# Two memory stacks, split operand tiles and ten plain columns of the feed-forward layer in a two-layer block of parallel heads

## The chip, the cores and the metric

The kernel runs on one core of one Trainium2 chip. TensorE multiplies matrices into PSUM; VectorE (DVE), ScalarE (ACT) and GpSimd (POOL) do the elementwise work; DMAs are issued from the queues of SP, POOL and ACT, each in its order. The metric is the device time of one launch in microseconds, as the median of several runs. All numbers are float32; matmul operands are split into a high part (type fp32r) and a low remainder, so one product costs three matmuls (high x high, high x low, low x high).

## The reference, cut to what matters

Two layers over 1024 tokens of width 1024. Each layer mixes tokens with four parallel heads and then applies a feed-forward part with a causal convolution of length 3 in its gate. Changed is only the feed-forward part of the second layer, and what lies around it.

```python
def conv_ffn(h, w_up, conv_w, conv_b, w_down):
    a, b = jnp.split(h @ w_up, 2, axis=-1)          # 1024 -> 2 x 2816
    a = causal_dwconv(a, conv_w) + conv_b.astype(a.dtype)
    return (jax.nn.gelu(a, approximate=True) * b) @ w_down

def hybrid_layer(x, ...):
    h = rms_norm(x, g_pre_mix)
    p = h @ w_in
    ...                                             # four mixers: pool, retention, gating, delta rule
    x = x + rms_norm(y @ w_out, g_post_mix)
    h = rms_norm(x, g_pre_ffn)
    x = x + rms_norm(conv_ffn(h, ffn_w_up, ffn_conv_w, ffn_conv_b, ffn_w_down), g_post_ffn)
    return x
```

## The kernel before

The tokens are worked on in two halves of 512 (`h` 0 and 1), the 2816 columns of the gate in 22 tiles of 128, called f. The code writes instructions in an order and with priorities (`high_priority` moves a block ahead); a scheduler of the compiler lays out each engine's order from that beforehand, with a simulated timeline, and also assigns buffers and semaphores. Each engine then runs its list in order. A tile that reuses memory waits for the last users of that memory.

The second layer's feed-forward part is done in two forms.

*Plain form* (`plain_up`, L1038): an f of half 0 takes two column tiles of w_up through `a_unit` (L205), each 8 k-steps x 3 matmuls of 512 columns, then `conv_gate` (convolution, gelu, product). Six f (`NPRE`) are done so for half 0. Two of them (`NFILL`) are filled into `win`, the mixers of half 1, the other four stand after it, before the output projection `out` of half 1. Each result c is stored to DRAM (`gD`, L1046). `plain_down` (L1048) loads it again with the rows of w_down, splits both and multiplies all six in one accumulation, for half 0 alone, and stores the sum (`accD`, L1079).

*Seven-product form* (`up_f`, L1133): both column tiles of an f are one 2 x 2 block product of 512 x 512 blocks, done with seven products and some sums instead of eight. `build` (L1099) loads the normalised rows `hn` from DRAM (`hnD`), forms four sums on POOL (L1109 to L1112), transposes seven blocks on TensorE (L1117), and writes their high and low parts (L1120, L1121) into the tiles A11, S1, S2, A12, S3, Q4, A22. Each such tile holds both token halves side by side, 512 columns; `build` is called once per half, with two token pairs per call. `up_f` loads the weights (`wraw`, L1140), casts seven weight blocks (L1145, L1146, added up by L1150), runs seven times `product` (12 matmuls each, L1129 to L1131), and gates. With `halves` (0, 1) a matmul has 512 columns, with (1,) it takes the 256 of half 1. The store of c goes from SP's queue (L1203).

The order at the end of the kernel is: `win` of half 1 with the fill; four more plain f; `out` of half 1, which ends in `norms` (L310) and the stores of hnD from SP's queue (L324); `plain_down`; `build` of half 1; f 0 and 1 for half 1; `build` of half 0; then f 2 to 5 for half 1, each in turn with one of f 6 to 21 for both halves; `down_full` (L1205), which loads w_down and gD per f (L1215, L1217), splits them, and multiplies in six groups, with the first two groups for half 1 alone and the sum of `accD` added.

Working memory is one stack of pools. `phase` (L135) closes all of them and opens the next set: the mixers' pools, then those of the seven products (`up_phase`), then those of `down_full` (`down_phase`).

```python
self.phase(("pw", 3), ("pr", NR), ("pa", 4), ("py", 2), ("pt", 5), ("ph", 4), ("pp", 1))   # mixers, plain form
self.phase(("pv", 2), ("pu", 1), ("pA", 1))                                                # seven products
self.phase(("pa", 8), ("py", 12), ("pw", 2), ("pr", 2), ("pg", 6))                         # down_full
```

Here pw holds weights, pr rows of 4 KB (`r4`), pa accumulators, ph transposed rows, pp the mixers' tensors, pv the weights of the seven products, pu the tags c (6 buffers: hn, sa, sb, a, c) and p, pA the A tiles, pg the split operands of `down_full`.

## Time and profile before

| | |
|---|---|
| median of 3 runs | 2526.12 us (2523.63 to 2530.67) |
| the profiled execution | 2522.4 us, span 2520.6 us |
| mean granted TensorE clock | 0.981 |
| TensorE busy | 2423.0 us, 96% of the span, 14020 matmuls |
| VectorE busy | 1777.1 us, 71% |
| ScalarE busy | 971.6 us, 39% |
| GpSimd busy | 251.7 us, 10% |
| DMA | 281.33 MB, mean 112 GB/s |

Times within the profile are microseconds from the start of the span. An arrow names what is written and what is read (`psg<-whi,hT` writes PSUM tile psg from whi and hT). After a bar stand busy time and mean length, after a second bar the idle time of the engine ahead of the group and what ended it. PEld is the loading of weights into TensorE, which overlaps its matmuls; SPq, POOLq and ACTq are DMA issues. The seven products run from about 1900 to 2291, `down_full` from 2303 to the end.

### The profile page before, as it was taken

What the parts mean: (1) busy time and instruction counts of PE and PEld (TensorE: products, weight loads), DVE (VectorE), ACT (ScalarE), POOL (GpSimd) and SP (SyncE); (2) the same over time, 40 slices, a digit from 0 to 9 for tenths busy, and PEclk for the clock granted to TensorE, in tenths of its full rate; (3) what the DMA queues carried; (4) which work ended last, traced back from release to release, by engine and by line L of the source; (5) the groups of instructions that cost most, each with busy time, mean ns of one, the idle gap of its engine ahead of it and who ended that gap; (6) DMA issues with size and microseconds to landing.
All of it is one profiled execution on the core that took longest, in us unless ns stands there. A gap on an engine that the chain in (4) does not pass through costs nothing.

```text
span 2520.6 us, 36318 instructions
## 1 busy us (share of the span) xinstructions
PE 2423.0 (96%) x14020; PEld 2023.0 (80%) x14020; DVE 1777.1 (71%) x3659; ACT 971.6 (39%) x1510; POOL 251.7 (10%) x351
## 2 busy tenths in 40 slices
PE   8989998999999999899999999989888999998998
PEld 7968887877788987787778898877767888886887
DVE  8895699765655888955565589886567876664547
ACT  6333452423333453342332255233345444434212
POOL 2321103000000022200000001211003000000000
PEclk9999999999999999999999999999898999998999
DMA  5233343322233552222222355323363222215424
GB/s 185 72 90 111 126 135 92 103 80 76 80 100 109 161 166 84 76 94 77 84 84 85 124 167 188 92 82 110 117 226 118 101 92 83 77 59 201 141 67 151
DMA packets 100496, 281.33 MB, mean 112 GB/s; under 512 B 30482, under 2 KB 30802, under 8 KB 99812
## 3 DMA queue, kind: packets, MB, share of 16 engines
q1 hardware_dynamic: 96548, 266.37, 32.2%
q0 software_dynamic: 3776, 12.65, 1.5%
q8 instruction: 110, 1.80, 0.3%
q14 instruction: 62, 0.51, 0.1%
HBM read 239.11 MB, written 39.88 MB: 111 GB/s over the span
## 4 chain that ended last, share of the span: by engine, by line
PE 77%; DVE 14%; DMA 3%; issue 3%; ACT 2%; POOL 0%; SPq 0%; DVEq 0%; ACTq 0%; POOLq 0%
PE psg L213 9%; PE psg L214 9%; PE psg L212 9%; PE psg L1286 3%; PE psg L1288 3%; PE psg L1287 3%; DVE pr L839 3%; PE psg L233 3%; PE psg L1129 3%; PE psg L1131 3%; PE psg L1130 3%; PE psg L234 3%; PE psg L235 3%; DVE wlo L203 2%; DVE A L841 2%
## 5 line engine op out<-in xcount | busy, mean ns | idle before, releaser
L212 PE MATMUL psg<-hT,whi 128*128 128x512 f32 x1248 | 496.4, 398 | 0.6 <-DVE rs L286 0.5
L213 PE MATMUL psg<-hT,whi 128*128 128x512 f32 x1248 | 496.4, 398 | 0.0
L214 PE MATMUL psg<-hT,wlo 128*128 128x512 f32 x1248 | 494.9, 398 | 0.0
L202 ACT CAST whi<-raw 128x1024 fp32r<-128x1024 f32 (+1 forms) x272 | 283.4, 1049 | 530.7 <-PE psg L213 217.8
L203 DVE TENSOR_TENSOR wlo<-raw,whi 128x1024 fp32r<-128x1024 f32 (+1 forms) x249 | 307.4, 1240 | 142.2 <-ACT whi L202 138.1
L213 PEld LDWEIGHTS psg<-hT,whi 128*128 128x128 f32 x1248 | 234.9, 188 | 54.5 <-issue 0.9
L214 PEld LDWEIGHTS psg<-hT,wlo 128*128 128x128 f32 x1248 | 235.0, 188 | 54.0 <-issue 0.4
L212 PEld LDWEIGHTS psg<-hT,whi 128*128 128x128 f32 x1248 | 235.2, 188 | 53.4 <-issue 1.3
L1293 DVE TENSOR_TENSOR acc<-acc,psg 128x512 f32<-128x512 f32 x160 | 108.9, 685 | 74.7 <-PE psg L1288 74.2
L1145 ACT CAST w<-wraw 128x512 fp32r<-128x512 f32 x154 | 92.7, 619 | 176.5 <-PE psg L1131 109.9
L234 PE MATMUL psg<-wlo,hT 128*128 128x256 f32 (+1 forms) x512 | 148.7, 291 | 4.8 <-DVE wlo L203 4.3
L233 PE MATMUL psg<-whi,y 128*128 128x256 f32 x512 | 143.9, 286 | 6.5 <-DVE raw L1018 2.8
L233 PE MATMUL psg<-whi,hT 128*128 128x256 f32 (+1 forms) x512 | 146.4, 290 | 2.3 <-ACT tmp L434 1.1
L235 PE MATMUL psg<-whi,hT 128*128 128x256 f32 (+1 forms) x512 | 148.0, 290 | 0.0
L234 PE MATMUL psg<-wlo,y 128*128 128x256 f32 x512 | 144.0, 284 | 0.8 <-DVE rv L295 0.8
L235 PE MATMUL psg<-whi,y 128*128 128x256 f32 x512 | 142.7, 283 | 0.0
L1286 PE MATMUL psg<-whi,g 128*128 128x512 f32 x352 | 141.5, 404 | 0.0
L1146 DVE TENSOR_TENSOR w<-wraw,w 128x512 fp32r<-128x512 f32 x154 | 105.0, 696 | 51.1 <-ACT w L1145 50.6
L1287 PE MATMUL psg<-wlo,g 128*128 128x512 f32 x352 | 138.8, 394 | 0.0
L1288 PE MATMUL psg<-whi,g 128*128 128x512 f32 x352 | 138.6, 394 | 0.0
L839 DVE SCALAR_TENSOR_TENSOR pr<-A 64x1 f32<-64x1 f32 (+30 forms) x124 | 110.4, 890 | 8.6 <-POOL A L835 6.4
L234 PEld LDWEIGHTS psg<-wlo,hT 128*128 128x128 f32 x512 | 98.4, 192 | 8.5 <-DVE wlo L203 5.1
(488 smaller groups left out, 5151.4 us busy)
## 6 DMA issues: line engine op xcount, KB each, us to landing
raw<-in_wU SPq DMA_DIRECT2D x100, 512.0 KB, 3.5
raw<-in_wA SPq DMA_DIRECT2D x56, 512.0 KB, 3.5
raw<-in_wD SPq DMA_DIRECT2D x50, 512.0 KB, 3.6
wraw<-in_wU SPq DMA_DIRECT2D x22, 1024.0 KB, 4.9
raw<-in_wO SPq DMA_DIRECT2D x40, 512.0 KB, 3.7
raw<-in_wB SPq DMA_DIRECT2D x24, 512.0 KB, 3.6
xs<-xb SPq DMA_DIRECT2D x24, 512.0 KB, 3.5
graw<-gD SPq DMA_DIRECT2D x22, 512.0 KB, 4.5
```

The lines of the kernel that those rows point to most:

```text
L202: nc.scalar.copy(hi[:, :n], raw[:, :n])
L203: eng.tensor_tensor(lo[:, :n], raw[:, :n], hi[:, :n].bitcast(F32), ALU.subtract)
L212: nc.tensor.matmul(ps, a[0], b[0], start=first, stop=False)
L213: nc.tensor.matmul(ps, a[0], b[1], start=False, stop=False)
L214: nc.tensor.matmul(ps, a[1], b[0], start=False, stop=last)
L233: self.nc.tensor.matmul(ps[:, :width], h0, hi[:, s], start=k == 0, stop=False)
L234: self.nc.tensor.matmul(ps[:, :width], h0, lo[:, s], start=False, stop=False)
L235: self.nc.tensor.matmul(ps[:, :width], h1, hi[:, s], start=False, stop=k == len(hT) - 1)
L839: V.scalar_tensor_tensor(pr[:, 0:i, 0:i], A[:, 0:i, 0:i], -1.0, A[:, 0:i, i].unsqueeze(1).to_broadcast([64, i, i]), ALU.mult, ALU.mult)
L1286: nc.tensor.matmul(ps, hi[:, tb], us[i][0][:, s], start=i == 0, stop=False)
L1287: nc.tensor.matmul(ps, hi[:, tb], us[i][1][:, s], start=False, stop=False)
L1288: nc.tensor.matmul(ps, lo[:, tb], us[i][0][:, s], start=False, stop=i == len(g0) - 1)
```

## The change

- The working memory becomes two stacks, a left and a right one. `layout(side, ...)` closes and opens one of them, so the pools of the next stage come in while the other side still works. The tags c (4 buffers instead of 6) and the loaded weights (two tiles of half the size, 3 buffers in a tag of pu) shrink with it.
- Each A tile is split by token half; `product` issues one matmul of 256 columns per half in place of one of 512.
- Ten f instead of six take the plain form for half 0. A generator, `plain_part`, yields after each pair of f: two up products, their gate split at once into pr tiles (no way through gD), and the down products of the pair before, added up in four accumulators. One step runs in the fill, two before `out`, the remaining ones after `build` of half 1 has been written.
- The stores of hnD and of the c of `up_f`, and the loads of hn, go from POOL's queue.
- `down_full` loads only the second half of gD for the ten plain f and has seven groups. The descriptor area for POOL's DMAs is 4096 instead of 8192 bytes.

```diff
-NPRE, NFILL = 6, 2
+NPRE, NMIX = 10, 2
...
+    def layout(self, side, *pools):
+        stack = self.stacks.pop(side, None)
+        if stack is not None:
+            stack.close()
+        stack = self.stacks[side] = ExitStack()
         for name, bufs in pools:
-            p = self.tc.tile_pool(name=f"{name}{self.nphase}", bufs=bufs, reuse_waits="tile")
+            p = self.tc.tile_pool(name=f"{name}{self.nphase}", bufs=bufs, side=side, reuse_waits="tile")
...
     def mix_phase(self):
-        self.phase(("pw", 3), ("pr", NR), ("pa", 4), ("py", 2), ("pt", 5), ("ph", 4), ("pp", 1))
-
-    def up_phase(self):
-        self.phase(("pv", 2), ("pu", 1), ("pA", 1))
+        self.layout("right", ("pw", 3), ("pa", 4), ("pr", NR), ("ph", 4))
+        self.layout("left", ("py", 2), ("pt", 5), ("pp", 1))
 
     def down_phase(self):
-        self.phase(("pa", 8), ("py", 12), ("pw", 2), ("pr", 2), ("pg", 6))
+        self.layout("right")
+        self.layout("left", ("pa", 8), ("py", 2), ("pw", 2), ("pr", 2), ("pg", 6))
...
-                    nc.sync.dma_start(keep[b * P:b * P + P], hn[b])
+                    nc.gpsimd.dma_start(keep[b * P:b * P + P], hn[b])
...
+    def plain_part(self, l, hT):
         nc, V = self.nc, self.nc.vector
         self.accD = self.pd.tile([HALF, D], F32, name="accD")
+        acc = self.acc_tiles()
+
+        def down(fs, gs):
+            us = [self.unit(self.t["wD"][l, f]) for f in fs]
+            for b in range(NB):
+                tb = slice(b * P, b * P + P)
+                for n in range(2):
+                    s = slice(n * 512, n * 512 + 512)
+                    ps = self.ps()
+                    for i in range(len(fs)):
+                        hi, lo = gs[i]
+                        nc.tensor.matmul(ps, hi[:, tb], us[i][0][:, s], start=i == 0, stop=False)
+                        nc.tensor.matmul(ps, hi[:, tb], us[i][1][:, s], start=False, stop=False)
+                        nc.tensor.matmul(ps, lo[:, tb], us[i][0][:, s], start=False, stop=i == len(fs) - 1)
+                    with self.tc.high_priority(offset=1500):
+                        if fs[0] == 0:
+                            nc.scalar.copy(acc[b][:, s], ps)
+                        else:
+                            V.tensor_tensor(acc[b][:, s], acc[b][:, s], ps, ALU.add)
+                if fs[-1] == NPRE - 1:
+                    nc.sync.dma_start(self.accD[tb], acc[b])
+
+        prev = None
+        for f0 in range(0, NPRE, GRP):
+            self.up = UF
+            fs = list(range(f0, f0 + GRP))
+            gs = []
+            cc = self.r4("c")
+            for i, f in enumerate(fs):
+                pa = self.a_unit(self.t["wU"][l, 2 * f], hT)
+                pb = self.a_unit(self.t["wU"][l, 2 * f + 1], hT)
+                with self.tc.high_priority(offset=1500):
+                    c = cc[:, i * HALF:i * HALF + HALF]
+                    self.conv_gate(l, 0, f, c, pa, pb)
+                    g = self.r4("g", F32R)
+                    self.split(g[:, :HALF], g[:, HALF:], c)
+                gs.append((g[:, :HALF], g[:, HALF:]))
+            if prev is not None:
+                down(*prev)
+            prev = (fs, gs)
+            yield
+        down(*prev)
+        yield
...
-        return self.pu.tile([P, 1028], F32, tag="c", name=name, bufs=6)
+        return self.pu.tile([P, 1028], F32, tag="c", name=name, bufs=4)
...
-                nc.sync.dma_start(x[:, :D], self.hnD[l][r0:r0 + P])
+                nc.gpsimd.dma_start(x[:, :D], self.hnD[l][r0:r0 + P])
...
+    def product(self, ps, n, b, halves, first, last):
         for k in range(4):
             s = slice(k * P, k * P + P)
+            for i, (x, y) in enumerate(((0, 0), (0, 1), (1, 0))):
+                for j, h in enumerate(halves):
+                    self.nc.tensor.matmul(ps[:, 256 * j:256 * j + 256], b[:, x, s], self.A[h][n][y][:, k, :],
+                                          start=first and k == i == j == 0, stop=k == 3 and i == 2,
+                                          skip_group_check=not first or j > 0)
...
-        raw = self.pv.tile([P, 4, 512], F32, tag="raw", name="wraw")
+        rb, ra = (self.pu.tile([P, 2, 512], F32, tag="raw", name="wraw", bufs=3) for _ in range(2))
...
-        nc.sync.dma_start(self.gD[l][f, :, halves[0] * HALF:halves[0] * HALF + 2 * N], c)
+        nc.gpsimd.dma_start(self.gD[l][f, :, halves[0] * HALF:halves[0] * HALF + 2 * N], c)
...
-        groups = [[0, 1], [2, 3, 4, 5], [6, 7, 8, 9], [10, 11, 12], [13, 14, 15, 16], [17, 18, 19, 20, 21]]
+        groups = [[0, 1], [2, 3, 4], [5, 6, 7], [8, 9], [10, 11, 12, 13], [14, 15, 16], [17, 18, 19, 20, 21]]
...
-                nc.sync.dma_start(r, self.gD[l][f])
+                o = HALF if f < NPRE else 0
+                nc.sync.dma_start(r[:, o:], self.gD[l][f, :, o:])
...
             def fill(a=acc):
-                keep["hT"] = self.to_hT(a, True)
-                self.plain_up(l + 1, 0, range(NFILL), keep["hT"])
+                keep["g"] = self.plain_part(l + 1, self.to_hT(a, True))
+                next(keep["g"])
...
-        self.plain_up(l, 0, range(NFILL, NPRE), keep["hT"])
+        part = keep["g"]
+        for _ in range(NMIX):
+            next(part)
         self.out(l, 1, y, True)
-        self.plain_down(l)
-        self.up_phase()
-        self.rows(l)
+        self.A = {}
+        self.layout("left", ("pu", 1), ("pA1", 1))
+        self.rows(self.pA1, 1)
         self.build(l, 1)
-        self.up_f(l, 0, (1,), 0)
-        self.up_f(l, 1, (1,), 0)
+        for _ in part:
+            pass
+        self.layout("right", ("pA0", 1), ("pv", 9))
+        self.rows(self.pA0, 0)
+        for f in range(2):
+            self.up_f(l, f, (1,))
         self.build(l, 0)
...
-                   dynamic_dma_scratch_size=8192)
+                   dynamic_dma_scratch_size=4096)
```

More of the change, by code (lines that the diff above doesn't have):

```diff
@@ L1036, in conv_gate @@
         V.tensor_tensor(c, c, pb, ALU.mult)
-    def plain_up(self, l, h, fs, hT):
-        self.up = UF
-        for f in fs:
-            c = self.pa.tile([P, HALF], F32, tag="acc", name="c")
-            pa = self.a_unit(self.t["wU"][l, 2 * f], hT)
-            pb = self.a_unit(self.t["wU"][l, 2 * f + 1], hT)
-            with self.tc.high_priority(offset=1500):
-                self.conv_gate(l, h, f, c, pa, pb)
-            self.nc.sync.dma_start(self.gD[l][f, :, h * HALF:h * HALF + HALF], c)
@@ L1095, in build, with sums @@
-    def build(self, l, h):
+            self.A[h][n] = [pool.tile([P, 4, 256], F32R, tag=f"{n}{x}", name=f"{n}{x}{h}") for x in "hl"]
+    def sums(self, xs, bufs):
+        L, R = slice(0, 512), slice(512, 1024)
+        s1, s2, q4, s3 = bufs
+        G = self.nc.gpsimd
+        G.tensor_tensor(s1, xs[1][:, L], xs[1][:, R], ALU.subtract)
+        G.tensor_tensor(s2, s1, xs[0][:, L], ALU.subtract)
+        G.tensor_tensor(q4, s2, xs[0][:, R], ALU.add)
+        G.tensor_tensor(s3, xs[0][:, L], xs[1][:, L], ALU.subtract)
+        return (("A11", xs[0][:, L]), ("S1", s1), ("S2", s2), ("A12", xs[0][:, R]), ("S3", s3), ("Q4", q4),
+                ("A22", xs[1][:, R]))
@@ L1096, in build, with turned, put @@
+    def turned(self, p, x):
+        for k in range(4):
+            self.nc.tensor.transpose(p[:, k * P:k * P + P], x[:, k * P:k * P + P], self.ident)
+        return p.rearrange("p (k t) -> p k t", k=4)
+    def put(self, n, p4, h, i):
+        cs = slice(i * P, i * P + P)
+        hi, lo = self.A[h][n]
+        self.nc.scalar.copy(hi[:, :, cs], p4)
+        self.nc.vector.tensor_tensor(lo[:, :, cs], p4, hi[:, :, cs].bitcast(F32), ALU.subtract)
+    def build(self, l, h, pairs=(0, 1)):
         nc = self.nc
-        V, A = nc.vector, self.A
@@ L1098, in build @@
-        for i in range(2):
-            cs = slice(h * 256 + i * P, h * 256 + i * P + P)
+        for i in pairs:
             xs = []
@@ L1123, in product @@
-    def product(self, ps, a, b, cs, first, last):
-        nc = self.nc
-        ah, al = self.A[a]
+            for j, (n, x) in enumerate(self.sums(xs, (sa[:, 0:512], sa[:, 512:1024], sb[:, 0:512], sb[:, 512:1024]))):
+                self.put(n, self.turned((self.ps, self.pq)[j % 2](), x), h, i)
+    def product(self, ps, n, b, halves, first, last):
         for k in range(4):
             s = slice(k * P, k * P + P)
-            st, sk = first and k == 0, not first
-            nc.tensor.matmul(ps, b[:, 0, s], ah[:, k, cs], start=st, stop=False, skip_group_check=sk)
-            nc.tensor.matmul(ps, b[:, 0, s], al[:, k, cs], start=False, stop=False, skip_group_check=sk)
-            nc.tensor.matmul(ps, b[:, 1, s], ah[:, k, cs], start=False, stop=k == 3, skip_group_check=sk)
+            for i, (x, y) in enumerate(((0, 0), (0, 1), (1, 0))):
[3 more added lines that the diff above has]
+                                          skip_group_check=not first or j > 0)
@@ L1179, in up_f @@
             nc.gpsimd.tensor_copy(a[:, 0:2], cf[:, f, :])
-        self.product(X, "A11", w11, cs, True, False)
-        self.product(Z, "S1", wt1, cs, True, False)
+        self.product(X, "A11", w11, halves, True, False)
+        self.product(Z, "S1", wt1, halves, True, False)
         with self.tc.high_priority(offset=1500):
@@ L1184, in up_f @@
             nc.scalar.copy(p5, Z)
-        self.product(X, "S2", wt2, cs, False, False)
-        self.product(W, "A12", w21, cs, True, True)
+        self.product(X, "S2", wt2, halves, False, False)
+        self.product(W, "A12", w21, halves, True, True)
         with self.tc.high_priority(offset=1500):
@@ L1189, in up_f @@
             V.tensor_tensor(p1, p1, W, ALU.add)
-        self.product(X, "S3", wt3, cs, False, False)
-        self.product(Z, "Q4", w22, cs, False, True)
+        self.product(X, "S3", wt3, halves, False, False)
+        self.product(Z, "Q4", w22, halves, False, True)
         with self.tc.high_priority(offset=1500):
@@ L1194, in up_f @@
             V.tensor_tensor(at[:, :, 0], v(Z), v(u2), ALU.subtract)
-        self.product(X, "A22", wt4, cs, False, True)
+        self.product(X, "A22", wt4, halves, False, True)
         with self.tc.high_priority(offset=1500):
@@ L1385, in run @@
         self.down_full(l)
-        self.stack.close()
+        for st in self.stacks.values():
+            st.close()
 _SHAPES = dict(
```

98 lines of the change are left out of this document (24 added, 74 removed).

## The prediction, made before the changed kernel ran

> **What bounds the kernel now.** I read the page first, then the table of stretches, then the waits of the stretches where TensorE stands still, then single rows for prices.
>
> ```profile
> span 2520.6 us, 36318 instructions
> PE 2423.0 (96%) x14020; PEld 2023.0 (80%) x14020; DVE 1777.1 (71%) x3659; ACT 971.6 (39%) x1510; POOL 251.7 (10%) x351
> ...
> PE 77%; DVE 14%; DMA 3%; issue 3%; ACT 2%; POOL 0%; SPq 0%; DVEq 0%; ACTq 0%; POOLq 0%
> ```
>
> TensorE is the bound nearly everywhere (77% of the chain that ended last), so a change can gain in two ways: fewer matmuls, or fewer of the few places where TensorE waits. This change adds matmuls, so its case rests on the waits. In the table of stretches the columns are length, busy time of PE, PEld, DVE, ACT, POOL, granted clock, DMA share, GB/s:
>
> ```profile
> 1730.00:1770.00 40.00, 40.00 (x415) 31.20 (x414) 24.82 (x55) 15.83 (x35) 3.64 (x12) 1.00 0.37 122
> 1770.00:1800.00 30.00, 21.90 (x146) 18.08 (x144) 17.41 (x59) 5.95 (x11) 3.90 (x11) 0.72 0.16 53
> 1800.00:1840.00 40.00, 38.32 (x313) 37.31 (x312) 24.96 (x52) 21.67 (x35) 0.00 (x0) 1.00 0.65 215
> 1840.00:1880.00 40.00, 36.36 (x144) 27.42 (x144) 21.37 (x58) 14.05 (x23) 0.00 (x0) 0.96 0.61 213
> 1880.00:1900.00 20.00, 9.32 (x43) 7.34 (x41) 16.30 (x24) 10.52 (x20) 7.53 (x6) 0.70 0.60 223
> 1900.00:1925.00 25.00, 23.98 (x196) 23.58 (x196) 20.82 (x36) 13.80 (x27) 4.44 (x5) 0.97 0.19 64
> 1925.00:1945.00 20.00, 15.03 (x89) 13.24 (x90) 14.06 (x24) 10.18 (x18) 11.55 (x11) 0.83 0.42 159
> 1945.00:2000.00 55.00, 55.00 (x320) 47.90 (x320) 43.04 (x68) 26.61 (x48) 0.95 (x4) 1.00 0.27 97
> 2290.00:2304.00 14.00, 1.43 (x6) 0.85 (x5) 5.61 (x6) 3.73 (x5) 0.00 (x0) 0.64 0.45 150
> ```
>
> I count as lost in a stretch its length less busy time times clock, since an idle TensorE also comes back at a lower clock. 1770:1800, the end of the scan: 30 - 21.90 x 0.72 = 14.2 us. 1840:1880, the plain down products: 5.1. 1880:1900, the first build: 13.5. 1900:1945, first products and second build: 1.7 + 7.5 = 9.2. 2290:2304, the step from up to down: 13.1. Together 55 us; the steady stretches around them lose nothing. What ended the waits (us in total, times, longest):
>
> ```profile
> PE psh L971 <- DVE tmp L625: 4.8, 2, 3.4
> ...
> ACT wbig L207 <- DMA raw<-in_wD: 5.2, 2, 3.9
> ...
> PE psg L1117 <- DMA hn<-hnD: 9.6, 3, 7.3
> ...
> PEld psg L1117 <- ACT w L1145: 7.7, 1, 7.7
> ```
>
> ```profile
> PE psm L1235 <- ACT g L207: 12.6, 1, 12.6
> ...
> ACT g L207 <- DMA wraw<-in_wD: 9.8, 3, 7.5
> ```
>
> So: a latency chain between VectorE and TensorE at the end of the scan, then normalised rows that go out to DRAM and come back (hnD), then weight loads that come late.
>
> **The change part by part.** Prices of a matmul are distances between starts, not durations, since durations overlap. The first pair of rows is 36 matmuls of 512 columns apart, the second 51 of 256:
>
> ```profile
> 2091.87 0.39 PE L1129 MATMUL psg<-A11h,w 128*128 128x512 f32 x1
> ...
> 2100.27 0.39 PE L1129 MATMUL psh<-A12h,w 128*128 128x512 f32 x1
> ```
>
> ```profile
> 1915.10 0.28 PE L1129 MATMUL psg<-S2h,w 128*128 128x256 f32 x1
> ...
> 1921.10 0.28 PE L1129 MATMUL psh<-A12h,w 128*128 128x256 f32 x1
> ```
>
> 8.40 us / 36 = 233 ns, 6.00 / 51 = 118 ns.
>
> *More plain f.* The four f from 6 to 9 leave the seven-product form for half 0. A plain half f is 2 units x 8 k x 3 = 48 matmuls of 512: 11.2 us. Their seven-product form was 84 matmuls of 512 for both halves, 19.6 us; now 84 of 256 for half 1, 9.9 us, plus 11.2: +1.5 us each, +6.0. Down products per f and half stay 24 matmuls, 5.6 us.
>
> *Operand tiles by token half.* For the 12 f that still do both halves each of 84 matmuls of 512 becomes two of 256: 2 x 118 - 233 = +3 ns a pair, x 1008 = +3.0 us. TensorE's work therefore grows by 9.0 us, all on the path.
>
> The Trainium skill speaks harder against this part: "TensorE: Matmul & The Clock Gate", section "Back-to-back issue gap", gives for a stream with weight loads about 81 ns at 128 columns and 131 ns at 512. Halfway in proportion, an estimate of mine, that is 98 ns at 256, so 65 ns a pair and +65 us in all. The rows above, which have their weight loads between them, say 3 ns.
>
> *Downs before the scan ends.* The fill of before, up products of f 2 to 5, runs out at 1770; its last c is stored at 1771.5:
>
> ```profile
> L1046 SPq DMA_DIRECT2D gD<-c x6: 320/326/338, 1693.3 to 1771.5; - x6
> ```
>
> The generator now adds the downs of f 0 to 3, 4 x 5.6 = 22.4 us, ahead of the output projection and independent of the scan. That is more than the 14.2 us lost. But every TensorE step of the scan then queues behind a few of them, so the chain ends later, and downs are evacuated on VectorE (below), the engine of the chain. Bounds: -14.2 (all filled) and 0 (the chain stretches as much as is filled). I take -11, because the same scan in 1730:1770, with fill, lost nothing.
>
> *Plain f behind the output projection.* In 1840:1900 18.6 us are lost: the down products wait for wD, and the build of half 1 waits for hnD, for sums on POOL, and for casts. Now f 6 to 9 (44.8 us of up) and the downs of f 4 to 9 (33.6) stand there, 78.4 us that need nothing of the projection; the gate's output goes straight into the split, with no trip through gD. From the first down product, right behind the projection, to the first product of the new form
>
> ```profile
> 1840.32 0.77 PE L1075 MATMUL psg<-whi,g 128*128 128x512 f32 x2 [0.64 <-ACT whi L207]
> ...
> 1899.78 0.58 PE L1129 MATMUL psh<-A12h,w 128*128 128x256 f32 x1
> ```
>
> it took 60 us, so the cover is 18 longer than what it covers. If it were gone, the 18.6 would return. Bounds -18.6 and -9 (as if a second, uncovered wait for casts of 7.7 us stayed, since the nine w tiles lie in memory that the plain tiles leave late). I take -16.5.
>
> *Second build.* Four buffers of tag c instead of six hold hn, hn, sa, sb of one token pair, so the second pair waits for the first, and all wait for a and c of the two half-f before them. The new rows of half 0 also need the memory of the weights and accumulators of the last plain downs.
>
> ```profile
> 1921.81 0.32 SPq L1203 DMA_DIRECT2D gD<-c  x1
> 1922.23 1.28 SPq L1104 DMA_DIRECT2D hn<-hnD  x2
> ...
> 1930.72 0.32 SPq L1203 DMA_DIRECT2D gD<-c  x1
> ```
>
> ```profile
> xb<-xs SPq DMA_DIRECT2D x16, 512.0 KB, 3.7
> ...
> hn<-hnD SPq DMA_DIRECT2D x8, 512.0 KB, 5.8
> xb<-xs POOLq DMA_DIRECT2D x8, 512.0 KB, 4.7
> ...
> gD<-c SPq DMA_DIRECT2D x12, 256.0 KB, 2.0
> ```
>
> ```profile
> L1109 POOL TENSOR_TENSOR sa<-hn x4: 1269/1272/1542, 1888.9 to 1935.2; 128x512 f32<-128x512 f32 x4
> ...
> L1121 DVE TENSOR_TENSOR Q4l<-psg,Q4h x4: 673/686/691, 1897.6 to 1944.6; 128x512 fp32r<-128x512 f32 x4
> ```
>
> Before, the loads sat on SP's queue behind the store of c. Now both are on POOL's queue: a store waits for its c, and behind it queue the loads, the sums and the small writes into a. The last buffer comes free when the second c has left (1930.7 + 2.0, plus 1.0 for POOL's queue by the two xb rows: 1934), then two sums, transposes, the second load (5.8 + 1.0) and four sums of 1.27: about 1949, where before the last row was written at 1945.3. So this stretch may lose 4 us more. Against that, casts for these f may run ahead under the last downs (ahead=2000 instead of 0), so the clock is up when it starts. Bounds -9 and +12 (a second full load and sums in the open); I take +1.
>
> On that 1.0 us the Trainium skill, "DMA: Bandwidth & Descriptors", section "Specifications", has about 1 us against 0.6 to the first byte; by it three transfers in this chain would cost 1.2 us instead of 3.0.
>
> *Up to down.* This is SP's queue at the seam:
>
> ```profile
> 2282.23 1.21 SPq L1217 DMA_DIRECT2D graw<-gD  x2
> 2295.21 0.32 SPq L1203 DMA_DIRECT2D gD<-c  x1
> 2296.31 0.32 SPq L1217 DMA_DIRECT2D graw<-gD  x1
> 2296.68 8.28 SPq L1215 DMA_DIRECT2D wraw<-in_wD  x3
> ...
> L1129 PEld LDWEIGHTS psm<-S1h,w x88: 187/188/197, 1902.9 to 2272.9; 128*128 128x128 f32 x88
> ```
>
> wD for the down stage was issued behind the store of the last c, after all products. With the store on POOL, and the load's memory now lying over S1 and A11 of half 1 (by the sizes in the code), it can leave once S1's last matmuls (2272.9) are through, some 15 us before the seam. What is late next: g of the second f lies over Q4 and A22, so its casts start at the last product; six partial sums of the first f (6 x 3 x 0.233 = 4.2 us) stand before it, and the accumulators lie where c was. Loads of gD are halved for ten f. Bounds -13.1 and -3; I take -11.
>
> *Smaller things.* Plain downs in twos rather than one group of six give 40 evacuations instead of 8, 32 of them adds:
>
> ```profile
> L1293 DVE TENSOR_TENSOR acc<-acc,psg 128x512 f32<-128x512 f32 x160 | 108.9, 685 | 74.7 <-PE psg L1288 74.2
> ```
>
> 32 x 0.685 = 22 us of VectorE, spread over some 140 us at 60%: hidden, unless it meets the normalisation; +1.5 (0 to +5). hnD and gD stores leave SP's queue, which frees weight loads behind them: in the terms above. The smaller descriptor area I cost at nothing, as POOL's transfers are few; with stalls it would lengthen the second build.
>
> Sum: +9.0 - 11 - 16.5 + 1 - 11 + 1.5 = -27 us. The profiled execution took 2522.4, the median of the runs shown is 2526.1; so 2495 beside the former and about 2499 as a median.
>
> **The rivals.** (1) *All covered.* The waits vanish and the second build is hidden by f 2: -14.2 - 18.6 - 9.2 - 13.1 + 9 = -46, 2480. For it: cover exceeds the loss at each place. Against it: TensorE's order is fixed beforehand, and the old order, too, had work (f 2) that did not fill the second build. (2) *The wait moves.* The second build, now on one queue with stores and four buffers, costs the +12 of its bound, and the scan keeps its 14 us: 9 + 0 - 16.5 + 12 - 11 + 1.5 = -5, 2521. For it: the rows of POOL's queue above; against it: 9.9 us of f 2 can stand there. (3) *The downs do not cover.* They are placed, but the projection and the norms run behind them in TensorE's queue, so the chain is as late as before: only the seam is gained, -11 + 9 = -2, 2524, no measurable change. (4) *Slower:* the split matmuls. If the 256-column pairs do not run at 235 ns, because weight loads then set the pace, each ns costs 1.0 us. It decides from 235 + 27 = 262 ns a pair; at the 188 ns that one load lasts, unhidden once a pair, it gives 2499 + 190 = 2689. For it: twice the loads in twelve f; against it: the 51 matmuls above, loads included.
>
> The Trainium skill's numbers ("Back-to-back issue gap", as above) would put rival 4 at 2499 + 62 = 2561; the trace speaks for 235.
>
> **How the numbers follow.** My forecast (2486 to 2512) 0.60; (1) 0.12; (2) 0.11, of which 0.07 within 0.3%; (3) 0.06; (4) 0.05; an order on TensorE that I don't see, slower, 0.06. A measurement of this kernel tells 0.3%, 8 us, from no change. Faster 0.60 + 0.12 + 0.04 = 0.76; same 0.07 + 0.06 = 0.13; slower 0.11. The range that leaves out two in ten reaches from (1) to (2), 2480 to 2522.
>
> **What would show it.** Right: 256-column products about 118 ns apart and no 512-column ones; TensorE at clock 1.0 from the scan to the first product, with downs in it; casts of A rows of half 1 under plain matmuls; wD of the down stage issued before the last product, and a seam of some 2 us. Wrong: pairs well over 235 ns; a hole of more than 12 us before the first product that uses A rows of half 0; the same hole before the projection with downs on both sides of it.

## The result: 31 us slower, and the profile after

The changed kernel took 2556.6 us (median; 2554.5 to 2557.6) against 2525.9 us for the kernel before on the same chip: ratio 1.012, interval 1.010 to 1.0135. I had forecast 2499. The page of the changed kernel, to set beside the one shown before the prediction:

```profile
span 2555.8 us, 38925 instructions
PE 2435.4 (95%) x15220; PEld 2093.1 (82%) x15220; DVE 1809.1 (71%) x3719; ACT 983.0 (38%) x1538; POOL 272.0 (11%) x389
PEclk9999998999999999999999999999969899999999
PE 75%; DVE 14%; DMA 4%; issue 4%; ACT 2%; POOL 1%; SPq 0%; DVEq 0%; ACTq 0%; POOLq 0%
```

The same row of clocks in the kernel before:

```profile
PEclk9999999999999999999999999999898999998999
```

A new 6 stands in the row of clocks where there was none: behind a standstill of TensorE the granted clock was low. The table of stretches shows where (length, busy time of PE, PEld, DVE, ACT, POOL, granted clock, DMA share, GB/s):

```profile
1737.00:1806.00 69.00, 67.38 (x461) 53.74 (x461) 45.41 (x113) 27.53 (x51) 6.46 (x20) 1.00 0.21 69
1806.00:1858.00 52.00, 47.71 (x383) 46.75 (x382) 31.30 (x63) 26.08 (x41) 0.54 (x1) 0.97 0.58 194
1858.00:1887.00 29.00, 0.00 (x0) 0.00 (x0) 16.33 (x49) 5.81 (x9) 2.66 (x5) 0.57 0.72 248
1887.00:1907.00 20.00, 13.39 (x59) 11.50 (x60) 8.85 (x13) 7.94 (x14) 11.46 (x12) 0.60 0.17 56
1907.00:1985.00 78.00, 77.70 (x337) 62.94 (x335) 40.61 (x53) 20.07 (x29) 0.00 (x0) 1.00 0.24 81
1985.00:2011.00 26.00, 21.73 (x166) 20.09 (x166) 21.79 (x39) 12.60 (x25) 1.65 (x3) 1.00 0.39 131
2011.00:2036.00 25.00, 12.45 (x61) 9.76 (x62) 19.05 (x27) 10.50 (x19) 13.05 (x12) 0.73 0.36 117
2036.00:2353.00 317.00, 317.00 (x2682) 317.00 (x2681) 223.44 (x344) 140.37 (x232) 15.88 (x38) 1.00 0.27 89
2353.00:2360.00 7.00, 2.54 (x11) 1.95 (x10) 5.84 (x7) 3.98 (x5) 1.05 (x2) 0.80 0.07 28
```

Row by row. 1737:1806 is the scan, with downs in it: 1.6 us lost. 1806:1858 is the output projection. Then 29 us with not one matmul, 20 us of transposes at clock 0.60, and only then, 1907:1985, the 78 us of plain f and downs that I had counted as the cover for exactly this. 2011:2036 is the second build: 25 - 12.45 x 0.73 = 15.9 us lost. From 2036 the products run without a gap. The single rows of TensorE at the hole:

```profile
1857.34 0.28 PE L237 MATMUL psg<-whi,y 128*128 128x256 f32 x1
1887.13 1.12 PE L1112 MATMUL psg<-ident,hn 128*128 128x128 f32 x4 [29.51 <-DMA hn<-hnD]
```

The last matmul of the projection is followed, in TensorE's fixed order, by the first transpose of the build of half 1. That needs hn, which is the projection's own result after the norms and a trip through DRAM (POOL's rows, with the store of the last block at 1880.27):

```profile
1880.27 0.53 POOL L326 DMA_DIRECT2D hnD<-osu  x1 [7.18 <-issue]
1880.88 1.05 POOL L1128 DMA_DIRECT2D hn<-hnD  x2
1888.46 1.26 POOL L1103 TENSOR_TENSOR sa<-hn 128x512 f32<-128x512 f32 x1 [6.52 <-DMA hn<-hnD]
```

The cover was ready by then: the first products of f 6 need hT, long there, and weights whose last high part was cast from 1861.1 (ACT's line for the casts in this stretch, the first of them still for the projection; the low parts on DVE followed by 1863.4):

```profile
L204 ACT CAST whi<-raw x4: 1031/1044/1050, 1852.4 to 1861.1; 128x1024 fp32r<-128x1024 f32 x4
```

The account, by the same matmuls in both profiled executions (spans 2520.6 and 2555.8, +35.2). Work is the number of matmuls times their pitch, the distance between the starts of neighbours: 233 ns for 512 columns, 118 for 256. The seam is the step from the products to the down stage.

| stretch | before | after | change | of it work | of it waits |
|---|---|---|---|---|---|
| start to a matmul at 1700, same work | | | +5.2 | 0 | +5.2 |
| from there to the projection's last matmul | | | +12.7 | +22.4 | -9.7 |
| to the first product | 60.3 | 126.9 | +66.6 | +44.8 | +21.8 |
| products | 390.8 | 369.2 | -21.6 | -36.1 | +14.5 |
| seam | 13.0 | 4.7 | -8.3 | 0 | -8.3 |
| down stage and end | | | -19.5 | -22.4 | +2.9 |

Work +8.7 (forecast +9.0), scan -9.7 (-11), seam -8.3 (-11): three terms came out. The term "plain f behind the output projection" was to give -16.5 and gave +21.8; the second build was to cost +1 and cost +14.5.

One price in this account is not even. In the profiled execution of the kernel before, the 256-column products of f 0 and f 1, from which the 118 was read, were mostly slow ones; over all of them the mean was 115.6 ns, against 118.3 in the changed kernel. With these means the work of the products is -34.1 and their waits +12.5, and the work of the whole change +10.7.

### The profile page after: what moved, and what is told of

Its sections match the earlier page's. It is cut to its first block, busy times and chain, and to the rows that moved or that the text cites. A ratio compares the mean times of both kernels' runs of the same rounds, so it can differ in the third digit from the quotient of the medians.

```text
span 2555.8 us, 38925 instructions
## 1 busy us (share of the span) xinstructions
PE 2435.4 (95%) x15220; PEld 2093.1 (82%) x15220; DVE 1809.1 (71%) x3719; ACT 983.0 (38%) x1538; POOL 272.0 (11%) x389
## 4 chain that ended last, share of the span: by engine, by line
PE 75%; DVE 14%; DMA 4%; issue 4%; ACT 2%; POOL 1%; SPq 0%; DVEq 0%; ACTq 0%; POOLq 0%
PE psg L215 9%; PE psg L216 9%; PE psg L214 9%; PE psg L1139 7%; PE psm L1139 4%; PE psg L1297 3%; PE psg L1298 3%; PE psg L1299 3%; DVE pr L841 3%; PE psg L235 3%; PE psg L236 3%; PE psg L237 3%; DVE wlo L205 2%; PE psh L1139 2%; DVE A L843 1%
## 5 line engine op out<-in xcount | busy, mean ns | idle before, releaser
L216 PE MATMUL psg<-hT,wlo 128*128 128x512 f32 x1312 | 524.1, 401 | 0.0
L215 PE MATMUL psg<-hT,whi 128*128 128x512 f32 x1312 | 523.4, 399 | 0.2 <-DVE hT L373 0.2
L204 ACT CAST whi<-raw 128x1024 fp32r<-128x1024 f32 (+1 forms) x290 | 301.9, 1048 | 570.6 <-PE psg L215 229.0
L214 PE MATMUL psg<-hT,whi 128*128 128x512 f32 x1312 | 518.9, 396 | 0.1
L205 DVE TENSOR_TENSOR wlo<-raw,whi 128x1024 fp32r<-128x1024 f32 (+1 forms) x267 | 329.2, 1239 | 171.5 <-ACT whi L204 166.7
L214 PEld LDWEIGHTS psg<-hT,whi 128*128 128x128 f32 x1312 | 250.4, 191 | 56.5 <-ACT tmp L436 0.5
L215 PEld LDWEIGHTS psg<-hT,whi 128*128 128x128 f32 x1312 | 247.8, 189 | 57.9 <-DVE hT L373 0.8
L216 PEld LDWEIGHTS psg<-hT,wlo 128*128 128x128 f32 x1312 | 247.5, 189 | 53.7 <-issue 0.4
```

Source lines behind the costliest of these rows:

```text
L204: nc.scalar.copy(hi[:, :n], raw[:, :n])
L205: eng.tensor_tensor(lo[:, :n], raw[:, :n], hi[:, :n].bitcast(F32), ALU.subtract)
L214: nc.tensor.matmul(ps, a[0], b[0], start=first, stop=False)
L215: nc.tensor.matmul(ps, a[0], b[1], start=False, stop=False)
L216: nc.tensor.matmul(ps, a[1], b[0], start=False, stop=last)
```

## Experiments

The kernels ran on several chips. The kernel before, run beside each, took 2524.2 to 2527.3 us, so a difference between two kernels from different chips is good to about 3 us.

### Is it the order, or are the operands late anyway?

Theory: order. Rival: hn's round trip and the casts of f 6's weights are late wherever the cover stands.

```diff
         self.A = {}
+        for _ in part:
+            pass
         self.layout("left", ("pu", 1), ("pA1", 1))
         self.rows(self.pA1, 1)
         self.build(l, 1)
-        for _ in part:
-            pass
```

> The changed kernel with the plain f 6 to 9 and the remaining down products issued ahead of the first build instead of behind it; nothing else differs. Theory (order): TensorE's fixed order has the 56 transposes of the first build directly behind the output projection, so it waits 29.7 us for hn with the cover standing behind that wait. Moved ahead, the hole between the projection and the first matmul after it falls below 5 us, the last transposes come at a clock above 0.9, and the time falls by 30 to 42 us, to 2515 to 2527. Rival (the operands are late in any order: the round trip of hn, and the casts of the weights of f 6 that queue behind the norms on DVE): a hole of over 15 us stays ahead of f 6 or ahead of the transposes, and the time falls by less than 15 us, to 2542 or more.

2524.8 us, 31.8 below the changed kernel (before: 2525.6; ratio 0.9999, 0.999 to 1.0009). The stretch that was empty, in this kernel:

```profile
1860.00:1940.00 80.00, 79.99 (x356) 64.85 (x355) 57.65 (x109) 28.03 (x43) 8.74 (x9) 1.00 0.50 173
1940.00:1955.00 15.00, 8.06 (x42) 6.54 (x42) 13.39 (x17) 6.78 (x13) 7.85 (x7) 0.64 0.35 119
1979.00:2007.00 28.00, 13.20 (x68) 11.46 (x67) 15.03 (x26) 10.80 (x20) 13.54 (x16) 0.63 0.38 131
```

The hole is gone, and the rival with it. Shown: the place of this loop, ahead of the build or behind it, cost the 31 us. But 15 - 8.06 x 0.64 = 9.8 us stay at the end of the first build (its last transposes came at a clock of 0.64, where I had expected 0.9), and the second build now loses 28 - 13.20 x 0.63 = 19.7.

With only one step of the cover ahead, the rest behind the build as it was:

```diff
         self.A = {}
+        next(part)
         self.layout("left", ("pu", 1), ("pA1", 1))
```

> The changed kernel with one step of the plain part (the first products of f 6 and f 7, 96 matmuls, and the down products of f 4 and f 5, 48) issued ahead of the first build; the rest stays behind it. 144 matmuls by 233 ns are 33.6 us, 4 more than the hole of 29.7. Theory (order, and only as much cover as the chain of hn is long): the hole closes to under 5 us and the time comes within 5 us of the kernel with the whole part ahead, 2515 to 2530. Rival (it needs the whole 78 us because the second pair of hn rows comes later, or because the copies of the build run against the casts for f 8 and f 9): the time is 8 us or more above the kernel with the whole part ahead.

2533.8 us, 9.0 above the whole part ahead: here the rival's time came out. 33.6 us of cover did not close a hole of 29.7, because the chain grew under it:

```profile
PE psg L1112 <- DMA hn<-hnD: 8.6, 2, 6.6
```

The first transpose came at 1897.7, 40 us after the projection, and the last store of hn went out at 1889.80 instead of 1880.27: the casts and additions of the cover run on DVE and ACT, where the norms run too. The hole measured beside idle engines was shorter than the same chain under cover.

### Do POOL's stores matter?

All stores and the loads of hn back on SP, the order left as in the changed kernel:

```diff
-                    nc.gpsimd.dma_start(keep[b * P:b * P + P], hn[b])
+                    nc.sync.dma_start(keep[b * P:b * P + P], hn[b])
...
-                nc.gpsimd.dma_start(x[:, :D], self.hnD[l][r0:r0 + P])
+                nc.sync.dma_start(x[:, :D], self.hnD[l][r0:r0 + P])
...
-        nc.gpsimd.dma_start(self.gD[l][f, :, halves[0] * HALF:halves[0] * HALF + 2 * N], c)
+        nc.sync.dma_start(self.gD[l][f, :, halves[0] * HALF:halves[0] * HALF + 2 * N], c)
```

> The changed kernel with all the stores of hn and of the gates and the loads of hn back on SP's queue; order of the engines' other work as the scheduler then gives it. Theory (order): the hole of 29.7 us behind the projection ends when the norms' chain on DVE does (1879.7) plus a round trip, so it stays within 26 to 33 us; the second build, whose loads then stand behind stores that wait for the gates, loses 0 to 15 us more, and the seam into the down stage opens again by 5 to 8: 2550 to 2580. Rival (POOL's queue delays hn): the hole shrinks by 8 us or more and the time falls below 2549.

2551.5 us, 5 below the changed kernel, with the hole at 27 us:

```profile
PE psg L1112 <- DMA hn<-hnD: 26.9, 1, 26.9
```

So POOL's queue is not the cause, though it costs some. The surprise is the seam, which did not open again: 4.5 us of wait, as in the changed kernel. That contradicts my seam term, so I put the gate stores on POOL in the kernel before, alone (the last line above, the other way round):

> The kernel before with the stores of the gates (gD) of the seven-product f on POOL's queue instead of SP's, nothing else. My forecast's seam term: the last store no longer stands ahead of the down stage's first wD load on SP, that load leaves before the last product, and the seam shrinks from 12.7 us of wait to under 6: 2514 to 2519. Rival (the memory of the down stage's first tiles sets it, which the stacks and their order decided, as the seam of 4.6 us with the stores back on SP suggests): the seam stays at 10 us or more, 2523 to 2529.

2529.7 us, 5.5 above the kernel before (ratio 1.0017, 1.0008 to 1.0026), and its seam grew:

```profile
PE psm L1235 <- ACT g L207: 15.4, 1, 15.4
```

12.6 before. The load of wD that this cast waits for was issued at 2297.62, a microsecond after POOL had issued the last gate store. Ahead of it in SP's queue no store was left, but the third load of gD (graw) was:

```profile
2297.25 0.32 SPq L1217 DMA_DIRECT2D graw<-gD  x1
2297.62 11.08 SPq L1215 DMA_DIRECT2D wraw<-in_wD  x3
```

```profile
2296.61 0.53 POOL L1203 DMA_DIRECT2D gD<-c  x1 [12.86 <-ACT g L207]
```

```profile
2296.00 1.22 DVE L208 TENSOR_TENSOR g<-graw,g 128x1024 fp32r<-128x1024 f32 x1
```

graw has two buffers in the code. The third load went out when the first buffer's split ended on DVE (2296.00 + 1.22 = 2297.22), and that split stood behind the gate of the last f. The kernel before does the same: that split ended at 2296.29, the third load went out at 2296.31, and wD behind it. In the changed kernel the load of wD goes out ahead of the loads of gD and before the last product (2353.3):

```profile
2339.46 0.33 SPq L1225 DMA_DIRECT2D wraw<-in_wD  x1
```

It leaves 0.03 us after the end of the last matmul that reads S1 (2339.43), and with the gate stores back on SP again 0.03 us after it (2332.99 and 2333.02, last product 2346.9). So it waits for S1's memory, as forecast, and the queue of the gate stores gave nothing. The early load needs two things: memory that comes free early, and a place in SP's order ahead of the loads of gD that wait longer. Neither was tried by itself.

### The two builds

Own buffers for the second build, in the right stack, on top of the part ahead:

```diff
-        self.layout("right", ("pA0", 1), ("pv", 9))
+        self.layout("right", ("pA0", 1), ("pv", 9), ("pz", 1))
...
-        self.build(l, 0)
+        self.build(l, 0, cbuf=lambda n: self.pz.tile([P, D], F32, tag="z", name=n, bufs=4))
```

> The kernel with the plain part ahead of the first build, and besides with four buffers of its own for the second build's rows and sums (in the right stack, where the pools of this stage leave the room), so that its loads need not wait until f 0 and f 1 give theirs back. Theory: the second build's loss of some 14.5 us comes from those buffers; its loads land during the plain part, the gaps between 2011 and 2037 of the changed kernel go, and the time is 9 to 15 us below the kernel with the part ahead alone, 2502 to 2515. Rival (the build is paced by the copies on ACT and DVE that make the A rows beside the casts of the weights): it gains under 4 us over that kernel.

2516.2 us, 8.6 below, a little under the theory's 9 to 15. In that kernel 44 of the first build's 56 transposes still stood behind the last down product, and the pool of PSUM tiles behind `ps` (psg) is shared with the downs. Transposes into the tiles of two other pools, psm and psh, instead:

```diff
-                self.put(n, self.turned((self.ps, self.pq)[j % 2](), x), h, i)
+                self.put(n, self.turned(self.pq("mh"[j % 2]), x), h, i)
```

> The kernel with the plain part first and own buffers for the second build, and the transposes of both builds in the PSUM tiles that the plain down products do not use (psm and psh in turn, no psg). There 44 of the first build's 56 transposes came behind the last down product, and the stretch from 1936 to 1951 lost 15 - 7.38 x 0.73 = 9.6 us. Theory: they waited in TensorE's order for psg tiles behind the downs, so now the first build lies under the downs and 7 to 11 us go: 2505 to 2509. Rival (the second pair's loads and sums on POOL, after buffers of the first pair, set the end): under 4 us, 2512 or more.

2501.5 us, 14.7 below, more than expected. Own buffers alone, then with the other PSUM tiles:

```profile
1936.00:1951.00 15.00, 7.38 (x41) 6.10 (x39) 13.93 (x17) 6.98 (x13) 7.85 (x7) 0.73 0.33 105
1971.00:1992.00 21.00, 13.03 (x85) 11.76 (x84) 18.55 (x32) 12.16 (x23) 8.34 (x10) 0.72 0.38 125
```

```profile
1936.00:1951.00 15.00, 13.18 (x85) 11.51 (x84) 10.43 (x17) 4.75 (x10) 0.00 (x0) 1.00 0.34 128
1971.00:1992.00 21.00, 17.67 (x134) 16.88 (x133) 19.01 (x33) 10.82 (x21) 1.38 (x3) 0.92 0.20 63
```

Lost: 9.6 + 11.6 against 1.8 + 4.7, 14.7 in all, as in the measured times (13.3 when each is taken against the kernel before on its chip). No transpose of the first build stands behind the last down product now. The second half I had not expected. The first build's end under the downs may free the second build, which follows it on POOL; but the same edit also takes the second build's own transposes out of psg, and the two were not tried apart.

Then the rows' stores (hnD) back on SP, the first of the three lines above:

> The same with the stores of the normalised rows hn back on SP's queue (loads of hn and stores of the gates stay on POOL). All on SP was 5 us faster than the changed kernel: 2.6 of it around 1500 to 1600 us, where the rows of half 0 are stored, and 2.6 in the hole. Theory: the rows' stores on POOL cost that, and with the hole covered the first 2 to 3 us stay to be gained. Rival: the 5 us came from the loads, or from execution to execution: within 1.5 us of the kernel with the stores on POOL.

2498.5 us, 3.0 below. The two profiled executions differ by 5.7 us: 4.3 of that stand before 1500 already, where both programs are the same, and 2.3 come between 1500 and 1600, as the theory has it. The size of the 3.0 is therefore not firm. This is the forecast's time, with the change's own parts, an order in which they work, and three small additions.

How much cover it needs, on the kernel with padding and all stores on SP that stands further below:

```diff
-NPRE, NMIX = 10, 2
+NPRE, NMIX = 8, 2
```

> The kernel with the padded right stack and all stores on SP, with eight plain f instead of ten. Two f less by 1.5 us each are 3 us of TensorE's work, and 33.6 us of cover behind the projection go (22.4 of first products, 11.2 of downs); 44.8 stay. The chain of hn from the projection's end took 29.7 us up to the first transpose and 20 for the build, 50 in all. Theory (order and length): cover ends some 5 us early, so it gains 3 and loses 3 to 8: 2491 to 2497. Rival (the work alone counts): 2487 to 2489.

2498.5 against 2491.2 with ten: +7.2 (8.0 when each is taken against the kernel before on its chip), just beyond the theory's range. 1900:1920 is where the shorter cover ends:

```profile
1900.00:1920.00 20.00, 12.46 (x76) 11.28 (x75) 18.45 (x25) 11.65 (x23) 8.46 (x8) 0.74 0.44 147
```

20 - 12.46 x 0.74 = 10.8 us lost there against 3 us of work saved.

### What the 256-column matmuls cost

The split of the operand tiles alone, in the kernel before, with `product` as in the change:

```diff
-            hi = self.pA.tile([P, 4, 512], F32R, tag=f"{n}h", name=f"{n}h")
-            lo = self.pA.tile([P, 4, 512], F32R, tag=f"{n}l", name=f"{n}l")
-            self.A[n] = (hi, lo)
+                self.A[h][n] = [self.pA.tile([P, 4, 256], F32R, tag=f"{n}{x}{h}", name=f"{n}{x}{h}") for x in "hl"]
```

> The kernel before with one thing of the change: operand tiles by token half, so that each matmul of 512 columns of the sixteen f that do both halves becomes two of 256. By the pitches (118 ns against 233) 16 x 84 pairs x 3 ns are +4 us: 2527 to 2533. Rival (weight loads set the pace of 256 columns): +65 ns a pair, +87 us, 2613. Below 2524 would mean that the tiles by half take a wait from the second build.

2517.3 us against 2524.2: ratio 0.9972 (0.9963 to 0.9982), faster where I expected +4 us. The same 100 us of products in the kernel before, with the split alone, and in the changed kernel:

```profile
2070.00:2170.00 100.00, 100.00 (x430) 80.59 (x429) 66.16 (x92) 40.37 (x61) 0.50 (x5) 1.00 0.22 79
```

```profile
2070.00:2170.00 100.00, 100.00 (x885) 100.00 (x884) 69.77 (x98) 43.20 (x64) 0.50 (x5) 1.00 0.25 90
```

```profile
2070.00:2170.00 100.00, 100.00 (x848) 100.00 (x847) 76.93 (x123) 48.18 (x83) 5.90 (x14) 1.00 0.31 103
```

430, 885 and 848 matmuls: 233 ns for 512 columns, 113 ns for 256 with the split alone, 118 in the changed kernel. The same instructions of the same shapes differ by 5 ns. First theory, that it lies in the place of their operands: multiples of 64 bytes, which the right stack's tiles had lost.

```diff
+        pad = ctx.enter_context(tc.tile_pool(name="pad", bufs=1, side="right"))
+        tc.nc.gpsimd.memset(pad.tile([P, 8], F32, name="pad"), 0.0)
         self.mix_phase()
```

> The kernel with plain part first, own buffers, psm and psh for the transposes and the rows' stores on SP, and besides 32 bytes of padding ahead of everything in the right stack. In the changed kernel the right stack's tiles (weights w, A rows of half 0) lie at addresses that leave 32 when divided by 64; in the kernel with the split alone all lie at multiples of 64, and there the 256-column products follow each other every 113 ns, in the changed kernel every 118. Theory (placement): the pitch falls to 113 to 114 ns; 12 x 168 + 10 x 84 = 2856 matmuls by 5 ns are 14 us: 2482 to 2487. Rival (two stacks, or the two pools far apart, set it, not the 32 bytes): the pitch stays at 118 and the time within 3 us of the kernel without padding, 2495 to 2501.

The same 32 bytes between `pA0` and `pv` only, and 32 bytes ahead of `pv` in the split kernel:

> The kernel without that padding (rows' stores on SP, psm and psh, plain part first, own buffers), but with 32 bytes between the A rows of half 0 and the weights, so that the weights w lie at multiples of 64 and the A rows of half 0 do not. If the weights' address sets the pitch: 113 ns, 2482 to 2487. If the streamed rows' address does: the pitch stays at about 118 for the rows of half 0 and is 113 for those of half 1, or 118 for all, 2490 to 2500.

> The kernel before with operand tiles by half, and 32 bytes of padding ahead of the pools of this stage, so that its weights and A rows lose the multiple of 64 that they had. Theory (placement): the pitch rises from 113 to 118 ns, 16 x 168 + 6 x 84 = 3192 matmuls by 5 ns are +16 us against the split alone, 2530 to 2536. Rival (not the address): 2514 to 2521.

2492.7, 2495.9 and 2517.3 us. The padding helped (865 matmuls in the same 100 us, 115.6 ns), but less than expected; and the split kernel without its multiple of 64 kept 113 ns and its time. The theory fell. Beside these, the kernel with padding and the gate stores on SP too:

> The kernel with 32 bytes of padding at the head of the right stack, and the stores of the gates back on SP, so that POOL's queue keeps only the loads of hn. My forecast gave these stores the seam of 11 us; the kernel before with them on POOL came out 5.5 us slower and its seam 2.8 longer. Theory (the seam hangs on memory, not on the queue): within 3 us of the same kernel with gate stores on POOL, seam 4.6 us as there. Rival (the forecast's): the seam opens to 10 or more and it takes 6 us more.

2491.2 us, 1.5 below the same kernel with gate stores on POOL and within its spread (2490.4 to 2496.2), and a seam of 4.5 us of wait: the queue of these stores does not matter.

Next theory: which of the two, weights or rows, lies higher in the partition.

```diff
-        self.phase(("pv", 2), ("pu", 1), ("pA", 1))
+        self.phase(("pA", 1), ("pv", 2), ("pu", 1))
```

> The kernel before with operand tiles by half, and the pools of this stage in another order: the A rows first (from 25 KB), the weights last (from 156 KB); in the kernel with the split alone the weights lie from 42 KB and the rows from 114. Theory (the weights' place high in the partition, as in the changed kernel from 135 KB, costs): the pitch rises from 113 to 117 or more. Rival (it does not depend on that): 113 to 114. The builds may take longer, since the rows' memory then lies over other tiles; only the pitch is read.

```diff
-        self.layout("right", ("pA0", 1), ("pv", 9), ("pz", 1))
+        self.layout("right", ("pv", 9), ("pz", 1), ("pA0", 1))
```

> The kernel with the padded right stack and all stores on SP, with the weights at the top of the right stack (192 to 229 KB) and the A rows of half 0 below them (119 to 176 KB), where they lay at 135 to 172 and 172 to 229. If the order of weights and rows in memory sets the pitch, it moves by 2 ns or more from 116 to 117, and the time by 6 us; if not, 2489 to 2494.

With the rows first the time was 2530.9 us and the pitch 120 ns, sharp:

```profile
2070.00:2170.00 100.00, 100.00 (x836) 100.00 (x835) 63.57 (x90) 39.39 (x60) 0.50 (x5) 1.00 0.21 75
```

With the weights on top the pitch stayed at 116 to 117, 2488.9 us. So not "higher" either. By the addresses in the compiled programs, though, the kernels fell into a row by the distance from the weights to the streamed rows modulo 1024: 192 in the split alone (113 ns, shifted or not), 0 with the rows first (120), 0 or 32 for half 0 and 928 or 960 for half 1 in the changed kernel and the padded ones (116 to 118). Three runs set that distance for both halves by padding alone, 96 bytes at the head of the right stack and 192, 64 or none between `pA0` and `pv`:

> The kernel with all stores on SP and a padded right stack, the padding chosen so that the streamed A rows of both halves lie 192 bytes behind the weights modulo 1024, as they do in the kernel with the split alone (2240 = 2 x 1024 + 192). Theory (distance within a power of two): the pitch goes from 116.5 to 113 ns for all, 2856 x 3.5 ns = 10 us, 2479 to 2484. Rival (something else): the pitch stays at 116 to 117, 2489 to 2493.

> The same with the rows 64 bytes behind the weights modulo 1024. If what matters is the distance modulo 128 (192 and 64 are the same there), as with 192: 113 ns, 2479 to 2484. If it is modulo 256 or more, a value between 113 and 120. Rival: 116 to 117 as without.

> The same with the rows at the weights' own place modulo 1024, distance 0 for both halves. Theory: 120 ns as with the rows first, 2856 x 3.5 ns = 10 us more than with the padding alone, 2499 to 2504. Rival: 116 to 117, 2489 to 2493.

Distance 192, 64 and 0:

```profile
2070.00:2170.00 100.00, 100.00 (x885) 100.00 (x884) 79.56 (x127) 48.56 (x84) 2.25 (x7) 1.00 0.31 105
```

```profile
2070.00:2170.00 100.00, 100.00 (x852) 100.00 (x851) 77.55 (x125) 48.26 (x83) 2.25 (x7) 1.00 0.30 99
```

```profile
2070.00:2170.00 100.00, 100.00 (x836) 100.00 (x835) 75.61 (x121) 47.49 (x82) 1.76 (x6) 1.00 0.30 103
```

113.0, 117.4 and 119.6 ns; the kernel with the rows first has the same count as the one with distance 0. Times 2480.9, 2490.1 (scattered, 2476 to 2494) and 2498.5 us: 17.6 us between 192 and 0, where 2856 matmuls by 6.6 ns make 18.9. This theory holds for 0 and 192, each in two different layouts.

The record bounds it on three sides. First, the distance alone does not fix the pitch. The kernel before has the same pools in the same order as the split alone, so its rows of half 1 also lie at 192. Of its unbroken groups of 12 matmuls of 256 columns, 19 ran at 113.5 to 114 ns and 17 at 117.5 to 118. The same product at the same clock of 1.00, first at 1.36 / 12 = 113 ns, then at 1.41 / 12 = 118:

```profile
1954.19 0.28 PE L1129 MATMUL psg<-S3h,w 128*128 128x256 f32 x1
...
1955.55 0.39 PE L1129 MATMUL psg<-S2h,w 128*128 128x512 f32 x1
```

```profile
1979.11 0.28 PE L1129 MATMUL psg<-S3h,w 128*128 128x256 f32 x1
...
1980.52 0.39 PE L1130 MATMUL psm<-S1l,w 128*128 128x512 f32 x1
```

Second, the program with distance 64 took 2476.3 us in one of its four executions and 2487.8 to 2494.4 in the others. The 117.4 ns is of one that took 2492.3. That 64 is always slow, and with it that the distance modulo 128 is refuted, is therefore not shown. Third, where half 1 lies at 960 and a product takes its rows alone, the pitch was 113 again (1.36 / 12, kernel with 32 bytes of padding):

```profile
2003.90 0.28 PE L1142 MATMUL psm<-S1h,w 128*128 128x256 f32 x1
...
2005.26 0.28 PE L1142 MATMUL psh<-A12h,w 128*128 128x256 f32 x1
```

At 928, in the changed kernel, most such products ran at 117 to 118. 960 and 192 are the same place modulo 256 and modulo 128. The period, and what sets the pitch beside the distance, stay open.

The kernel with distance 192 is the fastest: 0.983 of the kernel before (0.980 to 0.985), 46 us by the medians on the same chip.

## Why the prediction was wrong, step by step

**Plain f behind the output projection (forecast -16.5, bounds -18.6 to -9; measured +21.8).** The step that failed is "78.4 us that need nothing of the projection ... the cover is 18 longer than what it covers". The lengths were right and beside the point. I summed lengths and did not ask in which order TensorE would meet them. In the change the build is called ahead of the rest of the plain part, so its transposes come first in TensorE's order and the wait stands ahead of its cover. I wrote under rival 1 that TensorE's order is fixed beforehand, and gave "an order on TensorE that I don't see" six in a hundred; it was to be seen in the diff. The bound "-9" assumed that some cover always applies; the true bound was the whole chain uncovered, 29.7 us plus 20 of a throttled build.

**Second build (+1, bounds -9 to +12; measured +14.5).** The mechanism was right: four buffers, POOL's queue, two serial rounds. POOL's rows of the changed kernel:

```profile
2005.52 0.57 POOL L1213 DMA_DIRECT2D gD<-c  x1 [99.48 <-ACT w L1154]
2006.09 0.54 POOL L1128 DMA_DIRECT2D hn<-hnD  x1
2010.01 0.54 POOL L1128 DMA_DIRECT2D hn<-hnD  x1 [3.38 <-DMA gD<-c]
...
2024.26 0.56 POOL L1128 DMA_DIRECT2D hn<-hnD  x1
```

The size was off. The clock was up where the products began (1.00 in 1985:2011), but 4.3 us were lost there, against 1.7 in the kernel before, so the gain of casts that "may run ahead" did not come. The full second round of load and sums stood in the open, as the upper bound had it, with a clock of 0.73 on top that I had left out. By the stretches 4.3 + 15.9 us were lost, 9.2 before.

**Downs before the scan ends (-11; measured -9.7).** Right, mechanism and size; the row 1737:1806 shows it.

**Up to down (-11; measured -8.3).** The size was nearly right, the reason half wrong. The early load of wD came, and it came with S1's last matmul, as I had said. The store on POOL gave nothing: in the kernel before it cost 5.5 us, in the last kernels 1.5, within the spread. I read the last store of c as what held wD; the rows shown in the prediction have a load of gD between the two (2296.31), and behind that load wD still stood when the store was gone.

**More plain f and the split (+9.0; measured +8.7, or +10.7 by the means).** Right here by luck: +3 ns a pair holds at 118 ns, which I read from one stretch of the kernel before, while later groups there ran at 113; where the tiles lie otherwise the pitch is 113 or 120, -7 to +6 ns a pair. Rival 4 is refuted, and with it the estimate from the Trainium skill, "TensorE: Matmul & The Clock Gate", section "Back-to-back issue gap", of +65 ns a pair: the runs measure -7 to +6 (2 x 113 or 2 x 119.6 less 233).

**Smaller things (+1.5; measured +5.2 ahead of the change and +2.9 at the end).** Mostly not the change: programs that are the same up to 1500 us stood between 2.5 us earlier and 3.1 later there than the profiled execution of the kernel before. Between 1500 and 1600 us, where the rows of half 0 are stored, kernels with these stores on POOL lost 1.6 to 3.3 us, those with them on SP between -1.2 and +2.5. The +2.9 at the end I have not traced.

**The other rivals.** (1), all covered at 2480, needs the order put right, own buffers, other PSUM tiles and a good placement: 2480.9. (2) and (3) had the right suspects (a wait that moves to the second build, downs that do not cover), but a price that ended at the old time.

## To carry to other kernels

Cover works only if it stands ahead of the wait in the engine's own order: before summing lengths, write down what the in-order engine meets next after the last instruction that is ready, and look for shared PSUM or SBUF tiles that tie cover and covered together. Count the chain longer than the hole it leaves when idle, since the cover's casts and additions run on the engines of the chain (29.7 us became 40). When operand tiles are moved, compare the pitch of one unchanged group of matmuls before and after: it is a count in a window, and here it was worth 18 us. One group is not enough, though, since the same product ran at 113 and at 118 ns in one execution.

## What the runs showed of the hardware

In the profiled executions the pitch of back-to-back 256-column fp32r matmuls went with where the weights and the streamed rows lie to each other: 113.0 ns at a distance of 192 bytes modulo 1024, 117.4 at 64, 119.6 at 0, changed by padding alone. The distance does not fix it alone: at 192, in the kernel before, the same product took 113 and 118 ns, and the program with distance 64 took 2476 to 2494 us. Two 256-column matmuls at 113 ns were faster than one of 512 columns at 233 ns in the same place, with twice the weight loads. And an idle TensorE was paid twice: after the 29 us hole the 56 transposes of the build ran at a granted clock of 0.60.
